# A two-layer decoder trunk: exchanges moved to SyncE, a margin for side matmuls, x and p in other pieces

## Chip, cores, metric

The kernel runs on one core of one Trainium2 chip. The metric is device time in microseconds (us) of one execution, from the first instruction to the last. Three timed runs stand beside one profiled execution, and the trace is of that one.

## The reference

Two decoder layers on x of 512 tokens by 1024, in float32, and a last RMSNorm. Cut to what matters here:

```python
for i in range(2):
    hn = rmsnorm(x, norm_g[i])
    if i == 0: x = x + ab_mixer(hn, ...)     # 4 gated DeltaNet heads + 4 MoBA heads
    else:      x = x + fox_mixer(hn, ...)    # 8 forgetting-attention heads
    gate = sigmoid(rmsnorm(x, ple_norm_g[i]) @ w_ple_gate[i])
    x = x + gate * (p[i] @ w_ple_proj[i])
return rmsnorm(x, final_g)

# DeltaNet, per head and chunk of 64 tokens: G = cumsum(log decay)
a_mat = strict_lower((k_beta @ k.T) * exp(G_i - G_j))
u, w  = triangular_solve(eye + a_mat, [v * beta, k_beta * exp(G)])
# then a scan over the 8 chunks that carries a 128x128 state
# FoX: softmax(q.k/sqrt(d) + c_t - c_s) v, causal, c = cumsum(log f)
```

## The kernel before

**Tiling.** Activations stand transposed: eight tiles of 128 features by 512 tokens. A weight matrix comes in pieces of 1024 rows by 512 columns (two DMAs of 1 MB into the one `raw` buffer), and each piece is used in four chunks. A chunk is split into a rounded part `whi` (a copy on ACT or DVE) and a remainder `wlo` (a subtraction on DVE or POOL); three slots each hold them. Every product is three matmuls on such parts, so that a unit of 128 output features (`u`) takes 24 matmuls of 512 columns. Attention values come by rows (`vr`), the input embedding p by `pp`, the last gate by `fg`.

**The order of the work** is written by a planner (class `Plan`, from L123). It keeps a modelled time for each engine and for one DMA queue (`bw`, 2.8 us for 1 MB, a least time for names called `small`), and records instructions engine by engine in that order; the chip then runs each engine's list in order and waits on semaphores. There are two kinds of work. Main matmuls (`plan.main`: weights times activations) are recorded as soon as the model has their inputs ready. All other work runs in generators, the side work: transposes, attention, the DeltaNet parts, norms, splits, DMA issues. `pump` tries the generators in order of priority before each main matmul, and `fits` (L186) says whether a side instruction may be recorded now: for a side matmul (any instruction on PE) when its inputs are ready by the model at least 0.05 us before PE's modelled time. A side matmul that was recorded too early makes PE wait, and all main matmuls behind it.

**DMAs.** SyncE's queue (SP) issues weights, x, p and most spills to DRAM. ScalarE's own queue (ACTq) issues the small vectors, `w_ple_proj[0]` (into `bd`) and the exchanges through DRAM that the DeltaNet and the FoX gates need. A DMA issue stands in the list of its engine: if its data or its semaphore isn't ready, what is behind it on that engine waits too. The DMAs share eight semaphores, each used again only after its earlier DMA has landed.

**Start** (L382 to L394). p[0] comes as two DMAs of 256 KB (512-byte rows), `w_ple_proj[0]` as one of 1 MB, x as four of 512 KB. `load_pT` transposes p, `ple_cols` multiplies it by the projection (48 matmuls `pp`), `xload` transposes x (`xT`), `squares` and `rstd_x` form the norm: sums, Ln and Exp on ACT, a broadcast product `rx`, and in `normed` the scaled tiles `hn` with their parts `hhi` and `hlo`. The first units `u` need these.

**The DeltaNet exchange.** `gates` writes the cumulated decays to DRAM (`gd`) and reads them back four times, broadcast (`Gb`); `decays` takes the exponentials. `pair_products` makes `kn` per head and writes its 32x32 blocks to `kd` (16 DMAs). `inverses` reads them with one block per partition (`ub`), inverts them in 31 steps on DVE, writes the inverse and its transpose to `xd`, and reads them back as block diagonals (`bds`, 8 DMAs into `bd`). `wy` and `scan` (14 steps, each with the side matmuls `ws` and `su`) follow. In FoX, `fgates` writes `cd`, and `bias_c` reads it back for each head (`biasc`).

**Weight loads** (`Weights.loads`, L461): a load is issued as soon as `raw` is free, whatever else is under way. The rule of `fits` for side matmuls:

```python
        if op.eng == "PE":
            return now if w + 0.05 <= now else None
```

Of the kernel before, what the change touches and what calls it, by code (L numbers as in the profile page):

```python
# [122 lines left out]
class Plan:  # L123
# [32 lines left out]
    def emit(self, op):  # L156
        if op.name == "activation" and op.table() == LNEXP != self.table:
            self.emit(self.preload(LNEXP))
        w = self.when(op)
        assert w is not None, (op.name, op.r, op.w)  # L160
        start = max(self.t[op.eng], w)
        if op.locks():
            start = max(start, self.lock)
        c = op.cost(self)
        if op.table():
            self.table = op.table()
        self.t[op.eng] = start + c
        end = start + c
        if op.eng == "PE":
            end += 0.18  # L170
        elif op.name == "dma_start":
            o = op.outs[0] if op.outs[0].space != bass.MemoryType.DRAM else op.ins[0]
            b = o.nbytes if not callable(o.nbytes) else o.nbytes()
            small = any(n.startswith(("kd", "ub", "xd", "graw", "vrow")) for n in op.w + op.r)
            self.bw = max(end + 0.7, self.bw) + max(b / 1e6 * 2.8, 0.6 if small else 0.2) + 1.5 * ("graw" in op.w[0])
            end = self.bw + 0.9
        if op.locks():
            self.lock = end
        for n in op.w:
            self.ready[n] = end + self.SEM  # L180
        for n in op.r + op.w:
            d = self.last.setdefault(n, {})
            d[op.eng] = max(d.get(op.eng, 0.0), end)
        return op.f(*op.a, **op.k)  # L184

    def fits(self, op):  # L186
        w = self.when(op)
        if w is None:
            return None
        now = self.t["PE"]  # L190
        if op.eng == "PE":
            return now if w + 0.05 <= now else None
        if w > now + 0.3 or self.t[op.eng] > now + (1.0 if self.prio < 0 else 0.3):
            return None
        return max(w, self.t[op.eng], self.lock if op.locks() else 0.0) + op.cost(self)
# [122 lines left out]
def kernel(  # L318
# [60 lines left out]

    NV = 65  # L380
    vrow1, vrow = small("vrow1", [16, P]), small("vrow", [NV, P])
    prow0 = [t2("prow", shape=(P, NT, P)) for _ in range(2)]  # L382
    for c in range(2):
        do(SP.dma_start(prow0[c], p[0, 0, :, c * P:(c + 1) * P].rearrange("(t q) c -> q t c", q=P)))
    bd = [gp.tile([P, GH * NT * P], F32, name=nm("bd"), tag="bd", bufs=2)]
    ple0 = bd[0].rearrange("p (k c) -> p k c", k=2)
    do(A.dma_start(vrow1, norm_g.rearrange("i (f q) -> (i f) q", q=P)))
    do(A.dma_start(ple0, w_ple_proj[0].rearrange("(k q) c -> q k c", q=P)))
    xr = [plan.take("t4", "xr", (P, D)) for _ in range(NT)]
    for t in range(NT):  # L390
        do(SP.dma_start(xr[t], x[0, t * P:(t + 1) * P, :]))
    do(A.dma_start(vrow[17:65], conv_w[0].rearrange("k (f q) -> (k f) q", q=P)))
    do(A.dma_start(vrow[0:16], ple_norm_g.rearrange("i (f q) -> (i f) q", q=P)))
    do(A.dma_start(vrow[16:17], gdn_norm_g))  # L394
# [35 lines left out]
    class Weights:  # L430
# [30 lines left out]
        def loads(self):  # L461
            for i, views in enumerate(self.pieces):
                if views is None:
                    self.loaded.append(ple0)
                    continue
                raw = yield Slot("raw", "raw", (P, KT, 512))
                n = views[0].shape[1]
                for k, view in enumerate(views):
                    yield SP.dma_start(raw[:, k * n:(k + 1) * n], view)
                self.loaded.append(raw)  # L470
# [364 lines left out]
    def load_pT(i, rows, put, gate=None):  # L835

        if rows is None:
            yield gate
            yield Wait(lambda: plan.room("t2") >= 6)
            rows = []  # L840
            for c in range(2):
                r = t2("prow", shape=(P, NT, P))
                yield SP.dma_start(r, p[i, 0, :, c * P:(c + 1) * P].rearrange("(t q) c -> q t c", q=P))
                rows.append(r)
        for k in range(2):
            ps = yield Slot("B", "pT")
            for t in range(NT):
                yield T.transpose(ps[:, t * P:(t + 1) * P], rows[k][:, t, :], ident)
            hi, lo = t2("phi", F32R), t2("plo", F32R)
            yield copy(hi, ps)  # L850
            yield V.tensor_tensor(out=lo, in0=ps, in1=hi.bitcast(F32), op=ALU.subtract)
            free(ps)
            drop(rows[k])
            put((hi, lo))

# [135 lines left out]
    def gates(gps):  # L993
# [15 lines left out]
                                   op0=ALU.mult, op1=ALU.add)  # L1009
        drop(y, reset)  # L1010
        gd = dram.tile([GH, S], F32, name="gd")
        yield A.dma_start(gd, gb[0:4])
        Gb = []
        for hh in range(GH):
            b = t2("Gb")
            yield A.dma_start(b, gd[hh:hh + 1, :].to_broadcast([P, S]))
            Gb.append(b)

        ps = yield Slot("B", "gbT", (P, NT, P))
# [82 lines left out]
    def pair_products(hh):  # L1102
# [12 lines left out]
                                         in1=decay[hh][:, c], op0=ALU.mult, op1=ALU.mult)  # L1115
        free(ps)
        for bl in range(4):
            yield A.dma_start(kd[bl, hh].rearrange("t r c -> r t c"),
                               b.rearrange("p (t i) -> p t i", i=P)[bl * 32:(bl + 1) * 32, :,
                                                                    bl * 32:(bl + 1) * 32])  # L1120
        kn[hh] = b
# [19 lines left out]
    def inverses():  # L1141
# [3 lines left out]
        yield G.tensor_copy(vb.rearrange("p a b -> p (a b)")[:, 0:1024:33], ones[0:NB, 0:32])  # L1145
        yield Wait(lambda: len(kn) == GH)
        ub = yield Slot("t4", "ub", (NB, 32, 32))
        yield A.dma_start(ub, kd.rearrange("b h t r c -> (b h t) r c"))
        tmp = yield Slot("t4", "tmpb", (NB, 32, 32))
        for j in range(31, 0, -1):  # L1150
            n = 32 - j
            tv = tmp.rearrange("p a b -> p (a b)")[:, 0:j * n].rearrange("p (a b) -> p a b", b=n)
            if j == 10:
                flags.add("inv")
            yield [V.tensor_tensor(out=tv, in0=ub[:, 0:j, j:j + 1].to_broadcast([NB, j, n]),
                                   in1=vb[:, j:j + 1, j:32].to_broadcast([NB, j, n]), op=ALU.mult),
                   V.tensor_tensor(out=vb[:, 0:j, j:32], in0=vb[:, 0:j, j:32], in1=tv, op=ALU.subtract)]
        drop(ub, tmp)
        vbT = yield Slot("t4", "vbT", (NB, 32, 32))
        xd = dram.tile([2, 4, GH, NT, 32, 32], F32, name="xd")  # L1160
        yield A.dma_start(xd[0].rearrange("b h t r c -> (b h t) r c"), vb)
        yield V.tensor_copy(vbT, vb.rearrange("p a b -> p b a"))
        yield A.dma_start(xd[1].rearrange("b h t r c -> (b h t) r c"), vbT)
        drop(vb, vbT)
        for k in (0, 1):
            for bl in range(4):
                yield A.dma_start(bds[k][bl * 32:(bl + 1) * 32, :, bl * 32:(bl + 1) * 32],
                                   xd[k, bl].rearrange("h t r c -> r (h t) c"))
        flags.add("bds")

# [348 lines left out]
    def fgates(fps):  # L1519
# [8 lines left out]
        yield from softplus(yf, R)  # L1528
        yield G.memset(tl[R], 1.0)
        yield V.tensor_tensor_scan(out=cs[R], data0=tl[R], data1=yf[R], initial=0.0, op0=ALU.mult, op1=ALU.add)  # L1530
        yield A.dma_start(cd, cs[0:8])
        drop(tl, yf, cs)
        flags.add("cd")

# [2 lines left out]
    def bias_c(hh):  # L1537


        def make(b):  # L1540
            yield flag("cd")
            bias = yield Slot("t4", "biasc", (P, 8, P))
            yield A.dma_start(bias[:, 2:6, :], cd[hh:hh + 1, :].rearrange("h (b c) -> h b c", c=P).to_broadcast([P, 4, P]))
            yield G.tensor_copy(bias[:, 0, :], bias[:, 2, :])
            for i, dst in ((0, 1), (1, 7), (2, 6), (3, 5)):
                yield G.tensor_tensor(out=bias[:, dst, :], in0=bias[:, 2 + i, :], in1=cmask, op=ALU.add)
# [204 lines left out]
```

## Time and profile before

| | us |
|---|---|
| median of three runs | 740.1 |
| lowest, highest | 739.98, 744.07 |
| the profiled execution | 741.47 |
| its span in the trace | 739.7 |
| PE busy in it | 694.8 (94%) |
| DVE, ACT, POOL busy | 484.1, 330.5, 289.9 |
| mean granted TensorE clock | 0.984 |

The span is shorter than the execution's own time, since the trace begins with the first instruction. Busy times of PE include waiting in its pipeline; a stall shows in the timeline as idle time in front of an instruction, with the instruction or DMA that ended it.

### The profile page before, as it was taken

What the parts mean: (1) busy time and instruction counts of PE and PEld (TensorE: products, weight loads), DVE (VectorE), ACT (ScalarE), POOL (GpSimd) and SP (SyncE); (2) the same over time, 40 slices, a digit from 0 to 9 for tenths busy, and PEclk for the clock granted to TensorE, in tenths of its full rate; (3) what the DMA queues carried; (4) which work ended last, traced back from release to release, by engine and by line L of the source; (5) the groups of instructions that cost most, each with busy time, mean ns of one, the idle gap of its engine ahead of it and who ended that gap; (6) DMA issues with size and microseconds to landing.
All of it is one profiled execution on the core that took longest, in us unless ns stands there. A gap on an engine that the chain in (4) does not pass through costs nothing.

```text
span 739.7 us, 9095 instructions
## 1 busy us (share of the span) xinstructions
PE 694.8 (94%) x3324; PEld 570.1 (77%) x3324; DVE 484.1 (65%) x816; ACT 330.5 (45%) x623; POOL 289.9 (39%) x225
## 2 busy tenths in 40 slices
PE   5899999999899999989998999989999899999995
PEld 3688788878677778768886888867887777888884
DVE  2867785956755787877897444556346485776584
ACT  5536651225664364534443422436323355433445
POOL 3525375535542133045433254433444432535330
PEclk9899999999999999999998999999999899999998
DMA  7732534355311204143553035311244013344303
GB/s 262 275 84 96 172 88 125 103 143 150 54 53 36 79 1 171 53 146 130 198 185 115 28 115 140 97 48 41 74 143 113 29 29 104 111 171 156 114 1 114
DMA packets 51991, 80.42 MB, mean 109 GB/s; under 512 B 11085, under 2 KB 15518, under 8 KB 51946
## 3 DMA queue, kind: packets, MB, share of 16 engines
q1 hardware_dynamic: 43024, 74.00, 31.9%
q10 hardware_dynamic: 8922, 5.84, 2.8%
q8 instruction: 26, 0.43, 0.2%
q14 instruction: 19, 0.16, 0.1%
HBM read 68.53 MB, written 11.30 MB: 108 GB/s over the span
## 4 chain that ended last, share of the span: by engine, by line
PE 65%; DMA 13%; DVE 11%; POOL 4%; ACT 3%; issue 2%; ACTq 1%; SPq 0%; DVEq 0%; POOLq 0%
PE u L184 38%; PE vr L184 7%; DMA raw<-in_w_in_ab_dram 6%; DMA raw<-in_w_in_c_dram 4%; PE O L184 3%; PE fg L184 3%; POOL wlo L184 3%; PE pp L184 3%; PE PTp L184 2%; PE S L184 1%; DVE whi L184 1%; DVE gt L184 1%; DMA bd<-in_w_ple_proj_dram 1%; PE su L184 1%; DMA raw<-in_w_out_ab_dram 1%
## 5 line engine op out<-in xcount | busy, mean ns | idle before, releaser
L184 POOL TENSOR_TENSOR wlo<-raw,whi 128x1024 fp32r<-128x1024 f32 x79 | 197.7, 2509 | 324.7 <-ACT whi L184 238.3
L184 PE MATMUL u<-hlo,whi 128*128 128x512 f32 x480 | 191.7, 399 | 2.8 <-DVE hlo L184 2.8
L184 PE MATMUL u<-hhi,whi 128*128 128x512 f32 x480 | 192.0, 400 | 1.2 <-DVE vlo L184 0.9
L184 PE MATMUL u<-hhi,wlo 128*128 128x512 f32 x480 | 166.2, 402 | 0.4 <-POOL wlo L184 0.4
L184 ACT ACTIVATE whi<-raw 128x1024 fp32r<-128x1024 f32 x67 | 69.9, 1055 | 111.4 <-DMA raw<-in_w_in_c_dram 32.6
L184 PEld LDWEIGHTS u<-hlo,whi 128*128 128x128 f32 x480 | 91.3, 190 | 21.6 <-DVE hlo L184 4.1
L184 PEld LDWEIGHTS u<-hhi,whi 128*128 128x128 f32 x480 | 91.3, 190 | 19.7 <-DVE vlo L184 1.3
L184 PEld LDWEIGHTS u<-hhi,wlo 128*128 128x128 f32 x480 | 90.2, 190 | 18.3 <-POOL wlo L184 0.8
L184 PE MATMUL u<-yhi,whi 128*128 128x512 f32 x128 | 50.1, 392 | 2.8 <-ACT whi L184 2.8
L184 ACT ACT_TABLE_LOAD x36 | 46.2, 1283 | 12.8 <-DMA bd<-xd 4.4
L184 PE MATMUL vr<-whi,hlo 128*128 128x512 f32 x128 | 51.5, 402 | 0.0
L184 PE MATMUL vr<-wlo,hhi 128*128 128x512 f32 x128 | 51.4, 402 | 0.0
L184 PE MATMUL vr<-whi,hhi 128*128 128x512 f32 x128 | 51.4, 401 | 0.0
L184 PE MATMUL u<-ylo,whi 128*128 128x512 f32 x128 | 50.0, 391 | 0.8 <-DVE ylo L184 0.8
L184 DVE CAST whi<-raw 128x1024 fp32r<-128x1024 f32 x27 | 30.1, 1113 | 26.5 <-DMA raw<-in_w_in_ab_dram 9.3
L184 PE MATMUL u<-yhi,wlo 128*128 128x512 f32 x128 | 41.7, 390 | 0.0
L184 DVE TENSOR_TENSOR wlo<-raw,whi 128x1024 fp32r<-128x1024 f32 x15 | 29.6, 1975 | 14.2 <-ACT whi L184 14.2
L184 ACT ACTIVATE P<-P,nmx 128x128 f32<-128x128 f32 (+3 forms) x48 | 26.8, 559 | 21.6 <-DVE nmx L184 21.3
L184 ACT ACTIVATE hhi<-xres,vec 128x512 fp32r<-128x512 f32 x24 | 17.2, 721 | 39.9 <-DVE xres L184 39.9
L184 PE MATMUL PTp<-ident,P 128*128 128x128 f32 x120 | 24.9, 284 | 8.1 <-DVE P L184 6.7
L184 PEld LDWEIGHTS u<-yhi,whi 128*128 128x128 f32 x128 | 24.0, 188 | 8.5 <-ACT whi L184 3.2
L184 DVE SCALAR_TENSOR_TENSOR cacc<-u,vec,cacc 128x509 f32<-128x509 f32 (+2 forms) x36 | 26.4, 740 | 5.0 <-ACT cacc L184 4.8
(295 smaller groups left out, 1264.4 us busy)
## 6 DMA issues: line engine op xcount, KB each, us to landing
raw<-in_w_in_ab_dram SPq DMA_DIRECT2D x16, 1024.0 KB, 9.9
raw<-in_w_in_c_dram SPq DMA_DIRECT2D x16, 1024.0 KB, 7.6
raw<-in_w_ple_gate_dram SPq DMA_DIRECT2D x8, 1024.0 KB, 5.3
raw<-in_w_out_ab_dram SPq DMA_DIRECT2D x4, 1024.0 KB, 7.4
raw<-in_w_out_c_dram SPq DMA_DIRECT2D x4, 1024.0 KB, 6.2
xr<-in_x_dram SPq DMA_DIRECT2D x4, 512.0 KB, 8.8
x0d<-x SPq DMA_DIRECT2D x8, 256.0 KB, 8.4
ppd<-ppt SPq DMA_DIRECT2D x8, 256.0 KB, 4.4
```

Of the source, the lines that this page charges most:

```text
L184: return op.f(*op.a, **op.k)
```

## The change

It moves the exchange DMAs from ACTq to SP (`gd`, `Gb`, `kd`, `ub`, `xd`, `bds`, `cd`, `biasc`); holds a weight load back from step 4 of the inversion until the last `bds` DMA is issued; asks for 0.6 us in place of 0.05 us ahead of a side matmul; loads p in one DMA per layer, x in eight, `w_ple_proj[0]` in two; loads ACT's Ln and Exp table at the very start; sets the flag at which parked rows may be reloaded (`inv`) four steps sooner; and counts four more names as small transfers in the model.

```diff
-            small = any(n.startswith(("kd", "ub", "xd", "graw", "vrow")) for n in op.w + op.r)
+            small = any(n.startswith(("kd", "ub", "xd", "graw", "vrow", "bd_", "qd", "gd", "Gb")) for n in op.w + op.r)
...
         if op.eng == "PE":
-            return now if w + 0.05 <= now else None
+            return now if w + 0.6 <= now else None
...
-    prow0 = [t2("prow", shape=(P, NT, P)) for _ in range(2)]
-    for c in range(2):
-        do(SP.dma_start(prow0[c], p[0, 0, :, c * P:(c + 1) * P].rearrange("(t q) c -> q t c", q=P)))
+    prow0 = plan.take("whi", "prow", (P, NT, 2 * P))
+    do(SP.dma_start(prow0, p[0, 0].rearrange("(t q) c -> q t c", q=P)))
...
+    do(A.preload_act_table_set(LNEXP))
+    for c in range(2):
+        do(A.dma_start(ple0[:, :, c * 512:(c + 1) * 512],
+                       w_ple_proj[0, :, c * 512:(c + 1) * 512].rearrange("(k q) c -> q k c", q=P)))
     do(A.dma_start(vrow1, norm_g.rearrange("i (f q) -> (i f) q", q=P)))
-    do(A.dma_start(ple0, w_ple_proj[0].rearrange("(k q) c -> q k c", q=P)))
     xr = [plan.take("t4", "xr", (P, D)) for _ in range(NT)]
     for t in range(NT):
-        do(SP.dma_start(xr[t], x[0, t * P:(t + 1) * P, :]))
+        for c in range(2):
+            w = slice(c * S, (c + 1) * S)
+            do(SP.dma_start(xr[t][:, w], x[0, t * P:(t + 1) * P, w]))
...
+                yield Wait(lambda: "inv3" not in flags or "bds" in flags)
                 raw = yield Slot("raw", "raw", (P, KT, 512))
...
-            yield Wait(lambda: plan.room("t2") >= 6)
-            rows = []
-            for c in range(2):
-                r = t2("prow", shape=(P, NT, P))
-                yield SP.dma_start(r, p[i, 0, :, c * P:(c + 1) * P].rearrange("(t q) c -> q t c", q=P))
-                rows.append(r)
+            rows = yield Slot("t4", "prow", (P, NT, 2 * P))
+            yield SP.dma_start(rows, p[i, 0].rearrange("(t q) c -> q t c", q=P))
...
-        yield A.dma_start(gd, gb[0:4])
+        yield SP.dma_start(gd, gb[0:4])
...
-            yield A.dma_start(b, gd[hh:hh + 1, :].to_broadcast([P, S]))
+            yield SP.dma_start(b, gd[hh:hh + 1, :].to_broadcast([P, S]))
...
-            yield A.dma_start(kd[bl, hh].rearrange("t r c -> r t c"),
+            yield SP.dma_start(kd[bl, hh].rearrange("t r c -> r t c"),
...
-        yield A.dma_start(ub, kd.rearrange("b h t r c -> (b h t) r c"))
+        yield SP.dma_start(ub, kd.rearrange("b h t r c -> (b h t) r c"))
...
-            if j == 10:
+            if j == 14:
                 flags.add("inv")
+            if j == 4:
+                flags.add("inv3")
...
-        yield A.dma_start(xd[0].rearrange("b h t r c -> (b h t) r c"), vb)
+        yield SP.dma_start(xd[0].rearrange("b h t r c -> (b h t) r c"), vb)
...
-        yield A.dma_start(xd[1].rearrange("b h t r c -> (b h t) r c"), vbT)
+        yield SP.dma_start(xd[1].rearrange("b h t r c -> (b h t) r c"), vbT)
...
-                yield A.dma_start(bds[k][bl * 32:(bl + 1) * 32, :, bl * 32:(bl + 1) * 32],
+                yield SP.dma_start(bds[k][bl * 32:(bl + 1) * 32, :, bl * 32:(bl + 1) * 32],
...
-        yield A.dma_start(cd, cs[0:8])
+        yield SP.dma_start(cd, cs[0:8])
...
-            yield A.dma_start(bias[:, 2:6, :], cd[hh:hh + 1, :].rearrange("h (b c) -> h b c", c=P).to_broadcast([P, 4, P]))
+            yield SP.dma_start(bias[:, 2:6, :], cd[hh:hh + 1, :].rearrange("h (b c) -> h b c", c=P).to_broadcast([P, 4, P]))
```

## Rows read from the trace of the kernel before

**Rows 1.** The page's part 1: busy us, share of span, instructions.

```profile
PE 694.8 (94%) x3324; PEld 570.1 (77%) x3324; DVE 484.1 (65%) x816; ACT 330.5 (45%) x623; POOL 289.9 (39%) x225
```

**Rows 2.** Ten-us stretches: length, five engines' busy time (instructions), granted clock, DMA share, GB/s.

```profile
0.00:10.00 10.00, 2.60 (x9) 1.47 (x9) 1.33 (x4) 2.48 (x3) 3.38 (x21) 1.00 0.80 287
30.00:40.00 10.00, 7.65 (x21) 5.73 (x22) 10.00 (x11) 3.98 (x7) 7.79 (x11) 0.66 0.80 282
390.00:400.00 10.00, 6.90 (x28) 5.29 (x27) 9.27 (x10) 5.35 (x7) 5.63 (x2) 0.90 0.14 52
400.00:410.00 10.00, 10.00 (x38) 8.02 (x37) 3.97 (x7) 1.32 (x2) 0.06 (x1) 0.76 0.72 213
730.00:740.00 10.00, 1.07 (x10) 0.83 (x8) 4.59 (x17) 3.90 (x8) 0.00 (x0) 0.79 0.55 202
```

**Rows 3.** Waits of PE: who waited for whom, total us, times, longest.

```profile
PE PTp L184 <- DVE P L184: 6.7, 3, 3.6
...
PE tr L184 <- ACT cacc L184: 3.7, 2, 2.5
PE ssps L184 <- ACT sshi L184: 3.1, 1, 3.1
PE O L184 <- DVE PTlo L184: 3.1, 2, 2.3
PE u L184 <- DVE hlo L184: 2.8, 2, 1.8
...
PE PTp L184 <- ACT P L184: 1.3, 2, 0.7
PE su L184 <- DVE vn L184: 0.8, 2, 0.5
```

**Rows 4.** Timeline of PE at the start: start us, us, instruction [idle before].

```profile
11.53 0.80 PE L184 MATMUL pp<-phi,whi 128*128 128x512 f32 x1 [2.43 <-ACT whi L184]
```

**Rows 5.** The chain that ended last, at the start: start us, us, what.

```profile
1.22 9.18 DMA bd<-in_w_ple_proj_dram
```

**Rows 6.** Instructions on p's tile `prow`: its DMAs from issue to landing.

```profile
DMA to landing us min/median/max: 2.9/4.6/6.3
```

**Rows 7.** Timeline of ACT at the start.

```profile
10.42 2.00 ACT L184 ACTIVATE whi<-bd 128x1024 fp32r<-128x1024 f32 x2 [0.69 <-DMA bd<-in_w_ple_proj_dram]
...
22.01 1.28 ACT L184 ACT_TABLE_LOAD   x1
23.31 0.20 ACT L184 ACTIVATE xr<-xa 128x4 f32<-128x4 f32 x1
```

**Rows 8.** Timeline of ACT in the exchange.

```profile
118.25 1.29 ACT L184 ACTIVATE decay<-decay,nGp 128x128 f32<-128x128 f32 x4 [12.86 <-DMA kd<-kn]
189.39 1.28 ACT L184 ACT_TABLE_LOAD   x1 [4.44 <-DMA bd<-xd]
```

**Rows 9.** Timeline of SP's queue: the first weight load behind the `kd` issues.

```profile
126.76 0.93 SPq L184 DMA_DIRECT2D raw<-in_w_in_ab_dram  x2
```

**Rows 10.** Timeline of PE in the exchange.

```profile
191.37 0.66 PE L184 MATMUL tr<-ident,cacc 128*128 128x128 f32 x4 [2.52 <-ACT cacc L184]
```

**Rows 11.** The chain that ended last: two weight loads, the second beside the exchange.

```profile
149.14 9.95 DMA raw<-in_w_in_ab_dram
...
173.40 12.46 DMA raw<-in_w_in_ab_dram
```

**Rows 12.** DMA issues: out<-in, queue, count, KB each, median us to landing.

```profile
x2d<-xres SPq DMA_DIRECT2D x8, 256.0 KB, 2.0
...
xd<-vbT ACTq DMA_DIRECT2D x1, 256.0 KB, 8.4
```

**Rows 13.** Timeline of DVE: the last inversion step, and the held piece's first split.

```profile
173.01 0.18 DVE L184 TENSOR_TENSOR vb<-vb,tmpb 64x31 f32<-64x31 f32 x1
185.94 0.69 DVE L184 CAST whi<-raw 128x1024 fp32r<-128x1024 f32 x1 [2.13 <-DMA raw<-in_w_in_ab_dram]
```

**Rows 14.** Instructions on tile `su`: four matmuls a scan step.

```profile
L184 PE MATMUL su<-vn,kdc x56: 271/272/374, 232.4 to 281.8; 64*128 64x128 f32 x56
```

More of the change, by code (lines that the diff above doesn't have):

```diff
@@ L847, in load_pT @@
             for t in range(NT):
-                yield T.transpose(ps[:, t * P:(t + 1) * P], rows[k][:, t, :], ident)
+                yield T.transpose(ps[:, t * P:(t + 1) * P], rows[:, t, k * P:(k + 1) * P], ident)
             hi, lo = t2("phi", F32R), t2("plo", F32R)
@@ L852, in load_pT @@
             free(ps)
-            drop(rows[k])
             put((hi, lo))
+        drop(rows)
     pT = []
```

## The prediction

> **What bounds the kernel now.** Part 1 of the page comes first: PE is busy 694.8 us of a span of 739.7 [rows 1]. The other engines have a third of their time or more to spare, so what an edit can win is PE's idle time, 44.9 us, and the stretches in which PE runs at 1.2 instead of 2.4 GHz. The table by ten-us stretches says where these are: 7.4 us of idle time before the first ten us are over and 8.9 in the last ten, and 3.1 in 390 to 400; the rest comes in pieces of 1 to 4 us [rows 2]. It also prices a slow stretch: 390 to 410 has granted clocks of 0.90 and 0.76, so 10 x 0.10 + 10 x 0.24 = 3.4 us are lost there; and 30 to 40, at 0.66, loses 3.4 too. Both lie just behind idle time of PE. The waits of PE then tell whom PE waited for [rows 3]. Most of those lines are side matmuls (`PTp`, `tr`, `ssps`, `O`, `su`): they sum to 18.7 us. PE runs its list in order, so main matmuls stood behind each. Last come the timelines and the chain of waits around the edited places.
>
> **The start.** The first `pp` matmul starts at 11.53 [rows 4]. It waited for the split of `bd`, which began at 10.42 [rows 7] when that 1 MB landed, at 1.22 + 9.18 = 10.40 [rows 5]. Now p (0.52 MB) and the first half of the projection (0.52 MB) stand first on their two queues. The first ten us moved 287 GB/s [rows 2], and a quarter MB of p took 2.9 us to land at best [rows 6], of which 0.9 is its bytes at that rate, so 2.0 is fixed. 1.05 MB take 3.7 + 2.0 = 5.7 us; issued at 0.7, or at 2.0 if the new table load of 1.28 us holds ACT's issue back, they land at 6.4 to 7.7. With a copy of 1.0 us (2.00 for two [rows 7]), `pp` starts at 7.4 to 8.7, 2.8 to 4.1 us sooner. If the split waits for both halves of the projection, it begins behind some 2.3 MB (p, the projection, part of x), 8.0 + 2.0 + 0.7 to 2.0 = 10.7 to 12.0, and the term is nothing or a loss of about 1.5. I take -3.0, bounds -4 and +1.5: a DMA per half is what the split reads. The bytes up to the last of x are the same 3.7 MB, so x is not later.
>
> The gain counts only if the norm chain comes along, since the first units waited 2.8 us for `hlo` [rows 3]. That chain holds a table load at 22.01, which goes because the table is there from the start. The next ACTIVATE began at 23.31, 0.02 us after the load's 1.28 [rows 7], so the load's own time is all that leaves the chain: -1.3. Bounds: 0, if the planner shifts the units by as much, and -6.2, if both stalls (2.8) and the slow stretch behind them (3.4) go.
>
> The Trainium skill, page "ScalarE: Activation LUTs", section "What ACT_TABLE_LOAD costs", puts a switch of tables at 2.66 us, about half of it a drain. By that figure this term would be -2.7 and the sum -10.7; the trace shows no such drain here, and the row decides.
>
> **The exchanges leave ACT.** In the DeltaNet part ACT stood 12.86 us behind `kd` issues before the fourth head's `decay`, and 4.44 us behind `bd` issues [rows 8]. The first costs PE nothing that shows: units covered it. The second made `cacc` late, and PE idled 2.52 us at 191.37 for its transpose [rows 10]. With the issues on SP this wait goes: -2.5. Bounds 0 (the silu behind is late for another reason) and -3.7 (the other `tr` wait goes too [rows 3]). Late next is the weight piece, below. Behind the moved issues on SP stand weight loads, spills and reloads: a `kd` issue that waits for its head holds these back, but the next load on SP went out at 126.76 [rows 9], when ACT had been done with all but five of them for 8 us: nothing. `gd`, `Gb`, `cd` and `biasc` cost nothing: units run beside them.
>
> **The held load.** Before, the piece was issued as `raw` came free, at about 173, in the middle of the exchange, and took 12.46 us to land at 185.86 instead of 9.95 [rows 11]; its first split began at once, after a wait of DVE [rows 13]. Now it waits for the last `bds` issue. The last inversion step ends at 173.2 [rows 13]. The write of `xd` took 8.4 us beside the load; the nearest write alone, `x2d` of the same size, took 2.0 [rows 12]. Eight issues of about 0.45 us follow (0.93 for two [rows 9]), so the load goes out at 173.2 + 0.5 + 2.0 + 3.6 + 0.9 = 180.2 and lands, alone, at 190.2: 4.3 later than before. Against that the whole inversion starts sooner, because the fourth `decay` loses up to 12.86 us of waiting; its `kk` product and the weight load that `kd` lands behind remain, so I take 4, bounds 0 and 8. The load is then 0.3 us later, bounds -2 and 4.3. A late piece stops main work, but scan preparation and attention are there to run, so I take +1.5, bounds 0 and +8 (4.3 of delay plus a slow stretch of 3.4).
>
> **The margin.** A side matmul now comes 0.55 us later in PE's order, some two main matmuls. Each wait of rows 3 shrinks by 0.55 at most: `PTp` on DVE 3 x 0.55 = 1.65, the other `tr` 0.55, `ssps` 0.55, `O` 1.1, `PTp` on ACT 1.1, `su` 0.8 (all of it), together 5.75. The whole record is written anew, so some stalls will stand elsewhere: I take -4.0. Bounds: -9.2, if with the smaller wait at `ssps` its slow stretch goes too, and +3, since chains of side work get longer. The longest is the scan: 56 / 4 = 14 steps [rows 14], each with two side matmuls on its path, 28 x 0.55 = 15.4 us for both scans, or 7.7 where they run side by side. Units cover that, as does the earlier inversion; if that cover is gone, the output projection waits.
>
> The other edits (p[1] as one DMA, the reload flag, the names counted as small) cost nothing: units cover them, and their effect is the order that is counted above.
>
> **Sum.** -3.0 - 1.3 - 2.5 + 1.5 - 4.0 = -9.3. The profiled execution took 741.47, 1.8 over its span and 1.4 over the median of 740.1. Against that median the forecast is 730.8, given as **731**.
>
> **Rivals.**
> - **The stalls move** (chance 0.24). The planner's model is wrong by as much as before, and a new order brings new waits of 1 to 3 us. For it: the longest wait, 3.6 [rows 3], is far over 0.55. Then start and table remain, -4.3, at 736.
> - **Slow stretches go as well** (0.14). Shorter waits leave the clock up in these two places: -9.3 - 6.8, with rounding 724. For it: each slow stretch follows a stall of PE. Against: nothing shows how much shorter is enough.
> - **The held load is late** (0.11), the slower side. If the exchange takes as long on one queue as it did on two, the last `bds` issue stays at 189.4 and the load lands at 199.4, 13.5 us later; with 3.4 for the slow stretch and 4.3 off for the start this is 740.1 + 13.5 + 3.4 - 4.3 = 752.7, or 747 if side work covers 6. It decides from a load that lands more than some 9 us later. Against it: the 8.4 us came beside a load that is now held.
> - **The first split is no sooner** (0.06): both halves are waited for, and only the margin and ACT's freedom remain: 740.1 - 1.3 - 2.5 + 1.5 - 4.0 + 1 = 735.
> - **One queue costs what two did not** (0.05). In this kernel a `biasc` or `Gb` read would start behind a weight load of 9.95 us [rows 11] instead of beside it; up to 8 us for attention's first heads, of which units cover most: 736. The trace speaks against a large effect: `xd` took 8.4 us beside the load on a queue of its own [rows 12]. The Trainium skill, page "DMA: Bandwidth & Descriptors", section "Queues, rings and completion order", has each DMA engine take turns between queues packet by packet; by it ACT's reads had a share that SP's now lack.
>
> **How the numbers follow.** The forecast has 0.40, with its own range of 726 to 736. The range of 8 in 10 is **719 to 743**: down to the slow stretches' case with the larger start, up past the moved stalls and the smaller of the late loads. About 1%, 7.4 us, is what a measurement of this kernel can tell from no change: under 732.7 is faster, over 747.5 slower. Faster: 0.28 of the forecast, 0.14 of the slow stretches, 0.06 of the three rivals near 736, together 0.48, given as 0.5; slower 0.11; same 0.39.
>
> **What would show it.** Right: `pp` starts before 9 us; no `ACT_TABLE_LOAD` between the sums and Ln; no stall at `tr` behind `bd` issues; the held piece lands by 191 and PE is not idle for it; side waits of PE sum to under 13 us. Wrong: PE waits for `whi` after the exchange, `y` late after the scans, or as many side stalls as before.

## The result, and the profile after

The changed kernel takes 746.6 us (median of 15 runs, 742.39 to 747.44); the kernel before took 741.1 beside it (15 runs, 739.33 to 744.07). The ratio is 1.0063, with an interval of 1.0048 to 1.0079: slower by 0.6%, where 1.2% faster was forecast, and outside the range.

Part 1 of the page after: busy time and share of the span.

```profile
span 745.0 us, 9099 instructions
## 1 busy us (share of the span) xinstructions
PE 696.8 (94%) x3324; PEld 573.5 (77%) x3324; DVE 474.0 (64%) x806; ACT 339.6 (46%) x632; POOL 281.5 (38%) x223
```

The same 3324 matmuls keep PE busy for 2.0 us longer than in [rows 1], and its idle time is 745.0 - 696.8 = 48.2 us instead of 44.9. So 3.3 us of new waiting and 2.0 us more of busy time make the 5.3 us of span. The matmuls are the same, and the mean granted clock is 0.979 instead of 0.984, so I put the 2.0 us down to the clock.

Stretches of the kernel after, columns as in rows 2.

```profile
30.00:40.00 10.00, 9.84 (x44) 7.83 (x43) 10.00 (x12) 7.14 (x12) 10.00 (x5) 1.00 0.87 309
94.00:104.00 10.00, 7.13 (x39) 6.56 (x38) 8.07 (x18) 4.34 (x10) 8.42 (x11) 0.83 0.09 14
123.00:131.00 8.00, 5.97 (x15) 4.73 (x16) 5.83 (x3) 2.95 (x3) 5.94 (x3) 0.57 0.06 23
400.00:410.00 10.00, 7.49 (x26) 5.88 (x27) 6.28 (x10) 4.91 (x6) 2.37 (x1) 0.83 0.36 99
490.00:500.00 10.00, 7.01 (x26) 6.04 (x27) 4.86 (x11) 4.08 (x10) 6.50 (x11) 0.66 0.08 31
```

Against [rows 2]: the slow stretch at 30 to 40 is gone, though the first `pp` did not come sooner, and of the one at 390 to 410 half is left. New are 94 to 104 (0.83, so 1.7 us lost) and 123 to 131: 2.0 us idle and a clock of 0.57, so 8 x 0.43 = 3.4 us lost besides. 490 to 500 has become slow too (0.66, another 3.4). The kernel before had a third slow stretch, 570 to 590 (0.77 and 0.89), which the forecast left out.

Waits of PE after, columns as in rows 3.

```profile
PE u L184 <- ACT whi L184: 8.1, 2, 4.5
PE pT L184 <- DMA prow<-in_p_dram: 7.2, 1, 7.2
PE O L184 <- DVE PTlo L184: 4.7, 1, 4.7
PE O L184 <- ACT PThi L184: 3.9, 1, 3.9
PE pp L184 <- ACT whi L184: 3.5, 1, 3.5
PE ssps L184 <- ACT sshi L184: 3.1, 1, 3.1
PE kq L184 <- DVE kn L184: 2.9, 1, 2.9
...
PE tr L184 <- ACT cacc L184: 1.0, 1, 1.0
```

The small waits of [rows 3] are fewer: `PTp` on DVE (6.7) and one `tr` wait are gone. What stands now is fewer and longer. The waits for side matmuls sum to some 16.8 us instead of 18.7, and those for `whi`, the split of a weight piece, to 11.6 instead of 5.2.

How the two programs drift apart is seen from the start times of main matmuls, numbered in order. Main matmuls are here those of `pp`, `u`, `vr` and the gates. Each entry is us later (+) or sooner (-) than the same number in the kernel before; the last three rows are experiments told of below.

```
main matmul no.       72    288    360    576    936   1584   2016
starts before at    40.6   96.3  119.6  169.4  322.5  482.1  630.9
changed kernel      -1.6   +6.6   +9.1   +9.4   +6.2   +5.0   +5.1
e10                 -1.7   -1.2   +0.1    0.0   -8.8  -10.5  -10.1
e15                 -4.6   -4.4   -3.4   -3.6  -14.1  -16.0  -17.0
e17                 -4.8   -4.6   -3.3   -3.4  -12.2  -11.7  -24.2
```

The changed kernel is ahead at 40 us, and 9 us behind at 120. The whole loss is made in between, around the `kd` and `ub` exchange; nearly half of it comes back later.

**The start after.** Timeline of ACT (ACTq: its DMA issues).

```profile
0.71 1.28 ACT L184 ACT_TABLE_LOAD   x1 [0.71 <-PEq L1742]
0.74 1.03 ACTq L184 DMA_DIRECT2D bd<-in_w_ple_proj_dram  x2
1.80 0.49 ACTq L184 DMA_DIRECT2D vrow<-in_norm_g_dram  x1
6.75 0.33 ACTq L184 DMA_DIRECT2D vrow<-in_conv_w_dram  x1
8.15 0.32 ACTq L184 DMA_DIRECT2D vrow<-in_ple_norm_g_dram  x1
10.13 0.47 ACTq L184 DMA_DIRECT2D vrow<-in_gdn_norm_g_dram  x1
10.64 1.08 ACT L184 ACTIVATE phi<-pT 128x512 fp32r<-128x512 f32 x2 [8.65 <-DMA vrow<-in_conv_w_dram]
```

The first half of the projection landed at 6.73 and p at 7.09, inside the forecast's 6.4 to 7.7. But ACT stood at three small vector loads. The start now has 15 DMAs, which share eight completion semaphores, and each of the three is issued only when an earlier DMA on its semaphore, a piece of the projection or of x, has landed (at 6.73, 8.13 and 10.11). So ACT's first copy began at 10.64, and `pp` at 12.71 instead of 11.53 [rows 4].

**The exchange after.** Timeline of SyncE's queue from 97 to 116.

```profile
99.10 3.92 SPq L184 DMA_DIRECT2D kd<-kn  x8
103.12 0.85 SPq L184 DMA_DIRECT2D qd<-cacc  x2
105.13 1.74 SPq L184 DMA_DIRECT2D kd<-kn  x4
106.97 0.38 SPq L184 DMA_DIRECT2D qd<-cacc  x1
109.58 2.49 SPq L184 DMA_DIRECT2D kd<-kn  x4
112.18 0.94 SPq L184 DMA_DIRECT2D raw<-in_w_in_ab_dram  x2
113.22 0.45 SPq L184 DMA_DIRECT2D qd<-cacc  x1
113.85 1.00 SPq L184 DMA_DIRECT2D ub<-kd  x1
```

Between the issues SyncE waits for VectorE's `kn`, head by head. The fourth w_in_ab load comes behind them, at 112.18. In the kernel before it went out here, by the timeline of SP's queue:

```profile
102.86 0.92 SPq L184 DMA_DIRECT2D raw<-in_w_in_ab_dram  x2
```

Not all of the 9.3 us between is the queue's. The buffer `raw` came free with its last read, which in the timeline of POOL after is this:

```profile
105.85 2.37 POOL L184 TENSOR_TENSOR wlo<-raw,whi 128x1024 fp32r<-128x1024 f32 x1 [3.18 <-DVE oeps L184]
```

So `raw` was free at 108.22 (102.79 before), and the load stood 4.0 us in SyncE's queue. It landed at 123.84, and PE waited 4.54 us for its split at 125.03. `ub`, issued right behind the load on the same queue, landed at 125.08.

DMA issues: count, KB each, median us from issue to landing. The changed kernel; then e10 (`kd` alone back on ScalarE); then e4 (the hold made to hold).

```profile
bd<-xd SPq DMA_DIRECT2D x8, 64.0 KB, 6.8
kd<-kn SPq DMA_DIRECT2D x16, 16.0 KB, 1.5
ub<-kd SPq DMA_DIRECT2D x1, 256.0 KB, 11.2
```

```profile
bd<-xd SPq DMA_DIRECT2D x8, 64.0 KB, 2.6
kd<-kn ACTq DMA_DIRECT2D x16, 16.0 KB, 2.2
ub<-kd SPq DMA_DIRECT2D x1, 256.0 KB, 3.2
...
xd<-vbT SPq DMA_DIRECT2D x1, 256.0 KB, 3.1
```

```profile
bd<-xd SPq DMA_DIRECT2D x8, 64.0 KB, 2.4
...
xd<-vbT SPq DMA_DIRECT2D x1, 256.0 KB, 3.1
```

`ub` took 3.5 us in the kernel before, when no load was under way; it was issued later there and landed at 126.69, so the slow `ub` does not make the inversion late. Yet the first `xd` goes out at 180.57 instead of 173.92. The inversion's last three steps stand on VectorE behind the remainder of a weight piece, and that behind a split on ScalarE whose load landed at 168.47 (159.09 before). VectorE after, then before:

```profile
173.51 2.58 DVE L184 TENSOR_TENSOR wlo<-raw,whi 128x1024 fp32r<-128x1024 f32 x1 [10.06 <-ACT whi L184]
```

```profile
164.13 2.03 DVE L184 TENSOR_TENSOR wlo<-raw,whi 128x1024 fp32r<-128x1024 f32 x1 [7.04 <-ACT whi L184]
```

And the load that was to be held goes out at 182.87, between the two `xd` writes, so the exchange takes as long as before: from 180.57 to the last landing at 199.27 it is 18.7 us (17.5 before). PE has no wait over 1 us between 125.03 and 325.23, so neither costs it time.

### The profile page after: what moved, and what is told of

It is laid out like the page before. It is cut to its first block, busy times and chain, and to the rows that moved or that the text cites. A ratio compares the mean times of both kernels' runs of the same rounds, so it can differ in the third digit from the quotient of the medians.

```text
span 745.0 us, 9099 instructions
## 1 busy us (share of the span) xinstructions
PE 696.8 (94%) x3324; PEld 573.5 (77%) x3324; DVE 474.0 (64%) x806; ACT 339.6 (46%) x632; POOL 281.5 (38%) x223
## 4 chain that ended last, share of the span: by engine, by line
PE 69%; DMA 12%; DVE 10%; ACT 3%; POOL 3%; issue 2%; SPq 1%; DVEq 0%; ACTq 0%; POOLq 0%
PE u L184 39%; PE vr L184 10%; DMA raw<-in_w_in_c_dram 5%; DMA raw<-in_w_in_ab_dram 4%; PE O L184 3%; PE fg L184 3%; PE pp L184 3%; POOL wlo L184 2%; PE S L184 2%; PE PTp L184 2%; DVE gt L184 1%; ACT whi L184 1%; DVE wlo L184 1%; DMA bd<-in_w_ple_proj_dram 1%; DMA raw<-in_w_out_ab_dram 1%
## 5 line engine op out<-in xcount | busy, mean ns | idle before, releaser
L184 POOL TENSOR_TENSOR wlo<-raw,whi 128x1024 fp32r<-128x1024 f32 x75 | 188.5, 2518 | 365.9 <-ACT whi L184 298.2
L184 PE MATMUL u<-hhi,wlo 128*128 128x512 f32 x480 | 163.3, 397 | 0.3 <-POOL wlo L184 0.3
L184 ACT ACTIVATE whi<-raw 128x1024 fp32r<-128x1024 f32 x83 | 86.2, 1054 | 120.7 <-DMA raw<-in_w_in_c_dram 49.3
L184 DVE TENSOR_TENSOR wlo<-raw,whi 128x1024 fp32r<-128x1024 f32 x19 | 35.3, 1860 | 26.9 <-ACT whi L184 26.9
L184 ACT ACTIVATE P<-P,nmx 128x128 f32<-128x128 f32 (+3 forms) x48 | 26.7, 557 | 12.7 <-DVE nmx L184 11.8
L184 PEld LDWEIGHTS u<-yhi,wlo 128*128 128x128 f32 x128 | 24.0, 188 | 6.2 <-POOL wlo L184 1.3
L184 PEld LDWEIGHTS u<-ylo,whi 128*128 128x128 f32 x128 | 24.6, 192 | 5.1
```

## The experiments

Times are ratios to the kernel before, run beside each. Some experiments start from the changed kernel (1.0063), some from the kernel before (1).

**e1, the exchanges back on ScalarE** (changed kernel).

```
-  yield SP.dma_start(kd... / ub / xd / bds / gd / Gb / cd / biasc)
+  yield A.dma_start(...)                   # all nine
```

> The changed kernel with all nine exchange DMAs back on ACT's queue; start, margin, the hold's line and the model's names stay. Theory 1 (one ring): in the changed kernel `ub` took 11.2 us to land behind a weight load in SP's ring (3.5 before), and that load itself was issued at 112.2 behind `kd` issues though `raw` was free at 108.2; PE then waited 4.54 us for `whi` at 125 and ran slowly for 6.8 us. With the exchanges on ACT this stall goes: PE's idle time in 120 to 130 under 1 us, `ub` lands within 5 us, and the time falls by 5 to 8, to 739 to 742. Rival (the stalls are dealt anew by every edit, whichever it is): the stall at 125 goes but others of the same sum come elsewhere, 743 to 749. If ACT's own waits behind the issues cost what was forecast, a `tr` stall of 2 to 3 us comes back near 190.

Measured 1.0004 (0.9977 to 1.0032). The load went out at 103.17, `ub` took 3.6 us, and the wait near 117 was 1.86 us, without a slow stretch. The exchange edit costs 0.6% here. No wait for `tr` over 1 us came back near 190.

**e2, the old margin** (changed kernel; `w + 0.6` to `w + 0.05`).

> The changed kernel with 0.05 us in place of 0.6 us ahead of a side matmul, nothing else. Theory 1 (the margin works as priced, and other parts cost more than it gives): some ten side stalls grow by up to 0.55 each, PE's waits on side matmuls go from 16.8 us to 20 to 23, and the time rises by 3 to 6, to 750 to 753. Rival (the margin does nothing for the stalls, since they are of 3 to 5 us, from an ACT or DVE list that stands behind a weight load): waits on side matmuls stay within 3 us of 16.8 and the time within 743 to 749.

Measured 0.9961 (0.9932 to 0.999), 1% better with the margin out, and faster than either expectation. The waits are others: 5.14 for `PTp`, 4.16 for `O`, 3.63 for `whi`, 1.93 for `hlo`. Waits for side matmuls sum to 16.9 us against 16.8, where the first theory had 20 to 23. That the margin shortens waits by its size is refuted.

**e3, the old start and p[1] in two pieces** (changed kernel).

> The changed kernel with the start of before (p in two DMAs, the projection in one, x in four, no early table load) and p[1] in two. Theory 1 (the new start gains little because three small vector loads on ACT wait for semaphores that the pieces hold, so that the copies of p begin at 10.6 instead of about 8.3): `pp` starts at 11.5 again instead of 12.7, but the first units wait for `hlo` again with 2 to 3 us and a slow stretch; the first unit's 24th matmul comes 1 to 2 us later than in the changed kernel, and the time is 746 to 749. Rival (the new start costs time on the whole): 742 to 744.

Measured 0.9969 (0.9945 to 0.9994). `pp` starts at 11.28, and main matmul 72 comes 1.7 us sooner than in the changed kernel. The time is better than either theory had; the new start costs on the whole here, by more than those 1.7 us.

**e4, the hold behind the slot** (changed kernel).

```
-  yield Wait(lambda: "inv3" not in flags or "bds" in flags)
   raw = yield Slot("raw", "raw", (P, KT, 512))
+  yield Wait(lambda: "inv3" not in flags or "bds" in flags)
```

> The changed kernel with the line that holds weight loads moved behind the wait for the `raw` slot. Theory 1 (in the changed kernel the hold holds nothing, because the loads' generator passes it long before the flag and then stands at the slot): here the load of about 183 is issued behind the last `bds` issue, the exchange from the first `xd` issue to the last `bd` landing takes 8 to 11 us instead of 18.4, and the load lands 3 to 9 us later than at 194.3. PE had only 0.2 us of idle time between 130 and 290 in the changed kernel, so nothing is gained: 746 to 750. Rival (the exchange behind the load is what costs the changed kernel its time): 738 to 742.

Measured 1.0012 (0.9986 to 1.0039). Where the change put it, the wait is passed when the load before has been issued, long before the flag is set; with that line taken out, the program's instructions are the same on every engine. Behind the slot it holds: `xd` takes 3.1 us and `bd` 2.4, the exchange runs from 179.35 to 189.52, 10.2 us, and the load goes out at 188.45 and lands at 200.22. PE did not wait for it.

**e5, the exchanges alone on SyncE** (kernel before).

> The kernel before with one part of the change only: all nine exchange DMAs are issued by SyncE. One-ring theory (the exchange part costs by itself): ub lands about 11 us after its issue instead of 3.5, the load in front of it goes out late behind the kd issues, PE waits 3.5 to 4.5 us for whi between 115 and 126 and runs slowly behind it, ratio 1.002 to 1.007. Rival, the part is harmless and only the whole list of order changed: ub may be as late, but PE has no wait over 2 us there, ratio 0.996 to 1.000.

Measured 0.9987 (0.9967 to 1.0007). The load's first half went out at 106.40, between `kd` issues, its second at 109.51 behind them, and `ub` took 5.8 us; PE waited 1.76 us for `whi` at 119. So the part alone is harmless. That what it costs hangs on how long `kn` keeps SyncE is taken up behind e16.

**e6, the three vector loads on SyncE** (changed kernel).

```
-  do(A.dma_start(vrow[17:65], ...)), vrow[0:16], vrow[16:17]
+  do(SP.dma_start(...))                    # behind x
```

> The changed kernel with the three small vector loads (conv, ple_norm, gdn_norm) issued by SyncE behind x, so that ScalarE has no DMA issue left that can wait for a landing. Theory that these issues held ScalarE: the first copy phi starts at 7.2 to 7.6 instead of 10.64, the first pp matmul at 8.4 to 9.2 instead of 12.71, main matmul number 24 comes some 3 us sooner, ratio about 1.002. Rival one, the copy waits for bytes: phi no sooner than 10, ratio 1.006. Rival two, the start is sooner but the next waits eat it (x, the first held load, later stalls): pp at about 9, ratio 1.005 to 1.007.

Measured 1.0046 (1.0025 to 1.0068). Timeline of ACT:

```profile
0.71 1.28 ACT L184 ACT_TABLE_LOAD   x1 [0.71 <-PEq L1742]
...
8.15 0.60 ACT L184 ACTIVATE phi<-pT 128x512 fp32r<-128x512 f32 x1 [6.15 <-PE pT L184]
9.00 0.60 ACT L184 ACTIVATE phi<-pT 128x512 fp32r<-128x512 f32 x1 [0.26 <-PE pT L184]
```

The wait for the vectors is gone: `phi` at 8.15, `pp` at 10.2, main matmul 24 by 2.4 us sooner, and the profiled span ends 2.7 us sooner (742.3 against 745.0); the medians give 0.2%. `phi` is later than expected, since it waits for the transposes of p, and with it `pp`. The waits of 2.81 (`kq`) and 4.38 (`whi`) stand as before.

**e7 and e12, a margin of 0.10 and of 0.00** (kernel before, nothing else).

> The kernel before with a margin of 0.10 instead of 0.05 us for side matmuls and nothing else. Theory that any new recording of the order moves the long stalls by chance: at least two of the stalls over 1.5 us behind 100 us are gone or new, side waits sum to 13 to 24 us, and the time moves by 2 to 6 us to either side (ratio outside 0.998 to 1.002). Rival, the margin acts as a margin: the same stalls within 0.1 us, ratio 0.999 to 1.001.

> The kernel before with a margin of 0.00 instead of 0.05 us and nothing else. Theory that a new recording draws its long stalls by chance: stalls over 2 us behind 100 us are others than before and than with 0.10, and the time differs from before by 1 to 5 us to either side. Rival, a smaller margin is worse by its size: the same stalls, each 0.05 us longer, ratio 0.999 to 1.001.

Measured 1.0046 (1.0027 to 1.0065) and 0.996 (0.994 to 0.998). With 0.10 there are new waits of 3.30 at 117 (`whi`), 3.64 at 486 (`PTp`) and 3.12 at 526 (`O`); with 0.00 the long ones are the old ones but for a 2.68 at 605; the time is as the first theory had it, the waits are nearer the rival's. A change of 0.05 us to one number moves the time by 3 us to either side.

**e8, higher load times** (kernel before).

```
+  slow = 8.0 if w_in_ab, 6.1 if w_in_c, 5.0 for other weights
-  max(b / 1e6 * 2.8, ...)
+  max(b / 1e6 * slow, ...)
```

> The kernel before, with the order written out under landing times for weight loads as its trace shows them: 8.0, 6.1 and 5.0 us per MB for w_in_ab, w_in_c and the other weights instead of 2.8 for all; nothing else is edited. Theory that the long side stalls come from splits that stand in ScalarE's and VectorE's lists ahead of a landing the planner puts too early: PE's waits over 2.5 us for PTp, O and whi behind 300 us are gone, side waits sum to under 12 us, ratio 0.985 to 0.995. Rival, the stalls are of other making, or the planner only moves them to main matmuls: PE idles as long, ratio 0.997 to 1.005.

Measured 1.0392 (1.0359 to 1.0425). The waits for `PTp` and `O` over 1 us are gone, as the theory has it, and main matmuls now wait for splits: 18.5 us in 9 waits of `u` alone. The rival's mechanism holds, far beyond its range.

But these prices are not the trace's. The planner lays a piece's two DMAs end to end: by its formula the second, with nothing else under way, lands 0.7 + 2 x 1.05 x price + 0.9 us after its issue, which is 7.5 at 2.8, and here 18.4, 14.4 and 12.1. In the trace of the kernel before the second half landed after 9.9 to 12.5 us (w_in_ab), 9.0 to 12.3 (w_in_c) and 7.3 to 8.7 (w_out and the gate). So e8 prices every load 2 us or more too high, and it does not test what right prices would do.

**e9, the new start alone** (kernel before).

> The kernel before with one part of the change only: the new start (p as one DMA, the projection and x in halves, the early table load, the later p as one DMA). Theory that the part loses by itself, because ScalarE stands at three small vector loads: phi starts at 10 to 11, the first pp at 12 to 13, ratio 1.000 to 1.005. Rival from the prediction (start and table are worth 4.3 us): pp before 9, ratio 0.993 to 0.996. Rival, order by chance: pp late, and the ratio anywhere from 0.996 to 1.005 with long stalls behind 100 us in other places than before.

Measured 1.0078 (1.0054 to 1.0101): `phi` at 10.39, `pp` at 12.5, and waits of 2.94 at 121 and 4.49 at 323 for `whi` beside. It loses by itself, but not at the start: main matmul 72 comes 3.2 us sooner than in the kernel before, and number 288 still 0.5 sooner.

**e10, kd alone back on ScalarE** (changed kernel).

```
-  yield SP.dma_start(kd[bl, hh].rearrange("t r c -> r t c"), ...)
+  yield A.dma_start(kd[bl, hh].rearrange("t r c -> r t c"), ...)
```

> The changed kernel with the 16 kd issues alone back on ScalarE; ub, xd, bds and the rest stay on SyncE. Theory that the late weight load is SyncE's wait for kd's data: the fourth w_in_ab load goes out at 101 to 105 instead of 112.18, ub is issued behind its bytes and takes 3 to 6 us instead of 11.2, PE's wait for whi near 120 falls from 4.54 to under 2.5, ratio 1.000 to 1.003. Rival, the load is late for its buffer: it goes out after 108 and the wait stays over 3.5, ratio 1.005 to 1.008.

Measured 0.9836 (0.981 to 0.9863), far better than expected. Timeline of SyncE's queue from 97 to 128:

```profile
104.68 1.21 SPq L184 DMA_DIRECT2D raw<-in_w_in_ab_dram  x2
...
117.80 0.53 SPq L184 DMA_DIRECT2D ub<-kd  x1
```

The load is out 7.5 us sooner, `ub` finds the queue empty (3.2 us), and there is no wait for `whi` near 120. The second `xd` goes out at 165.05, the last `bds` piece lands at 171.93, and the next load goes out just then, at 171.87: the exchange is over 27 us sooner than in the changed kernel. Some of that is the order: here the inversion's last steps stand ahead of the late weight piece and end at 156.97, and so they do in e13, with `kd` on SyncE. The wait of `kq` is 0.67, that of `whi` at 312 is 1.43.

**e11, old margin, vectors on SyncE and a hold that holds** (changed kernel).

> The changed kernel with three edits together: margin 0.05 again, the three vector loads on SyncE, the hold behind the slot so that it holds. Theory that the parts' losses add: undone one by one they gave back 1.0, 0.2 and 0.5 per cent of the 0.6 that the change lost, so together ratio 0.990 to 0.994, with pp near 10, the xd writes under 4 us and no wait of kq. Rival, every recording draws its stalls anew: the three named signs are there, and the ratio still lies anywhere from 0.994 to 1.004.

Measured 0.995 (0.9925 to 0.9975): the signs are there (`xd` 3.1 us, no wait of `kq`), the sum of the parts is not.

**e13 and e14, the controls: a margin of 0.55** (e13 the changed kernel, e14 with `kd` on ScalarE).

> The changed kernel with a margin of 0.55 instead of 0.6 us and nothing else, a control for chance. Mechanism theory: the fourth w_in_ab load still goes out behind kd at 106 or later, ub takes over 9 us, PE waits over 2.5 us for whi near 120, ratio 1.000 to 1.009. Chance theory: the ratio falls anywhere from 0.985 to 1.009, with the load as late as in the changed kernel or not.

> The changed kernel with kd on ScalarE and a margin of 0.55, the control for e10. Mechanism theory: the load goes out before 106, ub takes under 6 us, no wait for whi over 2 us near 120, the last bds piece lands before 178, ratio 0.980 to 0.991. Chance theory: those signs may stand, and the ratio is 0.993 or more, because other stalls come up.

Measured 0.9984 (0.9965 to 1.0004) and 0.9897 (0.9869 to 0.9926). In e13 the load went out at 106.53, ahead of the last head's `kd`, so `ub` came after its bytes (3.3 us), and PE waited 3.91 us for `kn` at 97 instead of for `whi`: the signs that I expected of it failed but for the late load. In e14 the load went out at 101.23 and the wait for `whi` is 2.17, just over what was expected. `kd`'s place is worth 0.9% in this recording and 2.3% in the other; 0.05 us of margin is worth 0.8% to the changed kernel and costs e10's kernel 0.6%.

**e16, all exchanges but kd on SyncE** (kernel before).

> The kernel before with all exchanges but kd on SyncE; margin, start and load order as before. Mechanism theory: PE's wait for tr at 191 falls from 2.52 to under 1.2, xd still lands beside a weight load (no hold), ratio 0.990 to 0.998. Rival, kd's place is worth nothing by itself: within 0.2 per cent of all exchanges on SyncE (0.9987), 0.997 to 1.001.

Measured 1.0002 (0.9984 to 1.002). The `tr` wait at 191 is gone, but `xd` went out at 177.51 beside a load at 177.03. The rival holds: on the kernel before the split is worth nothing.

What `kd`'s place does to the fourth w_in_ab load can be read in every trace: us from the last read of `raw` to the load's issue, from there to the landing of its second half, and PE's wait for `whi` near 120.

```
kd on SyncE          e13   e5   e11   e2   changed   e4    e6    e3
issued after         0.9   1.5  2.1   2.4  4.0       4.1   4.2   4.3
landed after         12.6  13.1 13.7  14.6 15.6      15.7  15.8  15.8
wait for whi         none  1.76 2.69  3.63 4.54      4.56  4.38  4.20
```

With `kd` on ScalarE, in the twelve other kernels, the load goes out 0.2 us or less behind the last read and lands 11.3 to 12.3 us behind it. So the delay in the queue and the wait go together. The queue is not the only cause of such a wait: without it there are still waits from none to 3.30 (e7).

**e15, kd on ScalarE and the vectors on SyncE** (changed kernel).

> The changed kernel with kd on ScalarE and the three vector loads on SyncE. If the parts add: e10's 0.9836 less 0.2 per cent, 0.979 to 0.984, with pp near 10 and main matmul 24 some 2 us sooner than in e10. Rival, the order is drawn anew: pp near 10 and the ratio anywhere from 0.980 to 0.992.

Measured 0.9804 (0.9777 to 0.983). The parts add here, though the rival's range holds this ratio too: main matmul 72 comes 2.9 us sooner than in e10, and the lead is 6.9 us at main matmul 2016.

**e17 and e18, w_in_c loads at 4.2 and 6.1 us per MB in the order** (e15 and this one number).

> e15 with w_in_c loads written into the order at 4.2 us per MB instead of 2.8, every other load as before. Theory that the split stands too early in ScalarE's list: PE's waits for O at 472 and 562 (3.60, 4.59) shrink by 1 us or more each, main matmuls gain no wait over 1 us for whi, ratio 0.970 to 0.979. Rival, what is taken from the side work comes back at main matmuls, as with all prices in e8: PE waits for whi by 3 us or more in all behind 380, ratio 0.980 to 0.990.

> e15 with w_in_c loads at 6.1 us per MB, the price that the trace shows. Theory as in e17: no wait over 1 us for O or PTp behind 380, main waits for whi under 3 us in all there, ratio 0.965 to 0.978. Rival: the side waits go, and main matmuls wait for whi by 8 us or more behind 380, as in e8 (0.984 to 1.000).

Measured 0.9692 (0.9661 to 0.9722), a little better than the theory had, and 0.9833 (0.98 to 0.9866), between theory and rival. What they are about is seen in the changed kernel, ACT and then PE:

```profile
490.67 1.06 ACT L184 ACTIVATE whi<-raw 128x1024 fp32r<-128x1024 f32 x1 [7.44 <-DMA raw<-in_w_in_c_dram]
...
492.45 0.76 ACT L184 ACTIVATE PThi<-PTp 128x384 fp32r<-128x384 f32 x2
```

```profile
492.99 0.69 PE L184 MATMUL O<-PThi,vhi 128*128 128x384 f32 x1 [3.92 <-ACT PThi L184]
```

ACT stands 7.44 us at a split whose load has not landed, and the softmax work queued behind it (`PThi`) makes PE late. Waits of PE in e17:

```profile
PE ssps L188 <- ACT sshi L188: 3.2, 1, 3.2
PE PTp L188 <- ACT P L188: 1.6, 1, 1.6
PE u L188 <- ACT whi L188: 1.4, 1, 1.4
```

and in e18:

```profile
PE u L188 <- ACT whi L188: 6.3, 3, 2.4
PE vr L188 <- ACT whi L188: 5.2, 2, 2.8
PE vr L188 <- POOL wlo L188: 3.2, 2, 1.7
```

At 4.2 the waits for `O` (3.60 and 4.59 in e15) are gone, no main matmul behind 380 waits over 1 us for a split, and the granted clock is 0.996 over the span. By the formula under e8, 4.2 puts the second half's landing at 10.4 us, inside the 9.0 to 12.3 of the trace. 6.1, which I took for the price that the trace shows, puts it at 14.4: too late, the splits stand behind the softmax work, and main matmuls wait instead. e17 takes 717.5 us (716.85 to 720.41) and beats both kernels: PE is idle for 715.7 - 685.2 = 30.5 us.

## Why the prediction was wrong

- **The exchanges, and SyncE's queue.** This is the step that failed. I costed "Behind the moved issues on SP stand weight loads, spills and reloads" at nothing, from the load at 126.76 [rows 9]. The load that mattered is the one before it, issued at 102.86 among the `kd` issues and so in no row I read. Behind them it goes out at 112.18, 4.0 us after its buffer came free: 4.5 us of wait and 3.4 of slow clock at 123 to 131. That this is the queue's doing is shown by the rows behind e16. Just ahead of it PE waited 2.87 us for `kn` (at 99.13; 94 to 104 granted 0.83); VectorE was not waiting there but busy, 3.93 of the 4 us from 97 to 101. That wait is in e4, e6 and e13 too, and not in e1, e2 and e3, which differ from the changed kernel in unlike parts; its cause is not settled. e10 moves only `kd` and turns 1.0063 into 0.9836. The size is not settled: in the control (e13, e14) the same edit gives 0.9%, and on the kernel before (e5, e16) nothing. Main matmul 360, behind the exchange, comes 9.0 us later with `kd` on SyncE than on ScalarE in the first pair, 2.7 later in the second, and 2.5 sooner in the third. The wait of 2.52 at `tr` [rows 10] is gone, but as it is gone in e1 too, with the exchanges on ScalarE, the move alone is not shown to be its cause.
- **`ub` behind a load.** I expected little from one queue. `ub`, issued 1.2 us behind the load's second half on the same queue, landed 1.2 us after that load (125.08, 123.84); `xd`, issued 0.5 us behind one on the other queue, passed it in the kernel before (182.24, 185.85). The Trainium skill, page "DMA: Bandwidth & Descriptors", section "Queues, rings and completion order", says that an engine consumes a ring's descriptors in order and takes turns between rings; the traces agree. The same page, section "Issuing engines are not separate DMA queues", says that issuing from several engines "will only save the time on the sequencer"; here the queue also decides who lands first, 11.2 against 8.3 us for 256 KB.
- **The start (-3.0).** Wrong by sign for `pp`, which came 1.2 us later. The landings came as forecast; I counted the bytes and not the three small issues behind them on ACT. Nor did I count p's own way: with ACT free in e6, the transposes of p and the copies behind them still put `pp` at 10.2, not at 7.4 to 8.7. The slow stretch behind the start did go, which I had only as a bound, and so main matmul 72 is 1.6 us ahead, where start and table had -4.3. It goes with the old start as well (e3, 3.3 ahead), so the start's share is open: 1.7 us of loss against e3, 3.2 of gain in e9. What e9 loses in the end is lost at later waits.
- **The table (-1.3).** The load between the sums and Ln is gone; the term is not seen apart in the time. At 0.74 ACT's DMA issue went out during the table load of 0.71 to 1.99, so the 2.0 that I allowed was not needed.
- **The hold (+1.5).** Void, as no wait of the change reaches the load. Where e4 makes it hold its arithmetic comes near: 2.0 us forecast for `xd`, 3.1 measured; 7.0 from the end of the inversion to the load, 9.1 from `xd`'s issue measured; the load landed 11.8 us after that, where I had 10. The rival "late load" had the mechanism at the wrong load: it was the fourth that came late.
- **The margin (-4.0).** Wrong in kind. Side waits fell by 1.9, not 4, and with the margin out (e2) they sum to the same; the longest are new. Those for `O`, of 3 to 5 us, come from an in-order engine at a load that has not landed (e17), and 0.55 us does nothing for them. The rival "the stalls move" described it, at too small a price: e7, e12 and e13 show that any new recording is worth about half a per cent either way, more than most terms of my sum.

What stays open: how much of the 0.6% is chance. That the queue made the load late and PE wait is shown; that this decides the sign of the whole is not, since a neutral change moves the time as far. Every part undone alone made the changed kernel faster (e1 to e4, by 0.5 to 1.0%), and these do not add up (e11).

## What to carry to other kernels

When a DMA issue is moved to another engine's queue, list what is queued behind it there and when the data it waits for are ready; a queue that carries prefetches should carry no issue that waits for a compute engine. A hold must stand where the thing that it holds is decided, here behind the buffer and not before it. Where a program's order comes from a planner, time it under two or three neutral settings first: their spread is what an edit has to beat. And work out from the planner's own formula when a transfer lands before its price is changed: one price that fits gave 1.1% here (e17 against e15), one too high gave nothing (e18).

## What the runs showed of the hardware

A weight piece is two DMAs of 1 MB. In the kernel before the first landed 6.8 to 8.6 us after its issue and the second 9.9 to 12.5 for w_in_ab; for w_out 5.0 to 5.1 and 7.3 to 8.7. The 256 KB of `ub` or `xd` took 2.9 to 3.6 us alone, 7.0 to 8.5 beside a weight load on the other queue, and 9.8 to 11.2 when issued 0.8 to 2.6 us behind one on the same. ScalarE stood 4.5 us (2.29 to 6.75) at the issue of one small DMA, because an earlier DMA on the same completion semaphore had not landed.
